# A bidirectional recurrent branch with both directions' gate products first, both roots together and the squares in PSUM

## The chip, the cores and the metric

The kernel is one program on one core of a Trainium2 chip. The metric is the time of one execution on the device, in microseconds (us); less is better. The core's engines run at the same time, each through its own queue in order: PE (TensorE, matrix products), ACT (ScalarE, one function over a tile), DVE (VectorE, elementwise work and scans), POOL (GpSimd) and SP, whose queue issues most transfers. PEld is PE's loading of weights.

## The reference, cut to what matters

One encoder layer over 1024 positions of width 1024: a root-mean-square norm, an input projection, three mixers (a state-space one, a gated linear recurrence called RG-LRU, gated linear attention), three gates, an output projection, then an expert layer of 16 experts and a last norm. The change is in the RG-LRU, 512 channels wide and run in both directions:

```python
def rg_lru_direction(xc, w_a, b_a, w_x, b_x, lam, reverse):
    r = sigmoid(blockdiag(xc, w_a) + b_a)
    i = sigmoid(blockdiag(xc, w_x) + b_x)
    log_a = -LRU_C * r * softplus(-lam)
    a = exp(log_a)
    mult = sqrt(maximum(-expm1(2 * log_a), 0))
    # h[t] = a[t] * h[t-1] + mult[t] * i[t] * xc[t], forwards or backwards in t
    _, h = lax.associative_scan(_lin_combine, (a, mult * (i * xc)), reverse=reverse, axis=1)
    return h

def rg_lru_mixer(xb, ...):
    xc = conv(xb, conv_w, width 4, per channel) + conv_b
    return rg_lru_direction(xc, ..., reverse=False) + rg_lru_direction(xc, ..., reverse=True)
```

## The kernel before

Activations lie with channels on the 128 partitions and the 1024 positions along the free axis. To keep 32-bit accuracy each operand of a large product is split into a high and a low part (`split`: a copy on ACT at L54, a subtraction on DVE at L62), and `mm3` (L68 to L70) adds three products. A projection column of 128 channels (`proj`, L380) takes 48 matmuls into a two-bank PSUM tile `pj`, of which there are two; a branch's way up to the full width (`up`, L390) takes 6 matmuls for each 128 channels of the branch, and 24 for the RG-LRU's 512.

The RG-LRU is a Python generator, `lru_gen`. It goes over four chunks `c` of 128 channels. For a chunk, `lru_conv` loads the row block `xcl`, forms the convolution `xc` on DVE (one multiply, three multiply-adds, one addition of the bias at L897) and splits it into `xch` and `xcl`. Then the body goes over the two directions `d`. A direction has four gate products into `mx` tiles (one PSUM bank each, four of them for the whole program at this stage), four Tanh on ACT into `lr` and `li`, a Tanh into `lt`, an Exp in place over `lr`, a Square into `ls`, on DVE `lt = (ls + 1) * lt` and a maximum with 0 (L928), a square root on ACT, two multiply-adds into `li`, and the scan (L934). `lr` has two buffers; `li`, `lt`, `ls`, `xc`, `xch` and `xcl` have one each. At the end of a chunk the two scans are added and split into the pair `y`, an operand of the way up.

The generator doesn't run alone: `drive(gates_gla, lru_gen(), 6)` writes one task and then six steps of the generator, in turn. The tasks are eight `gla_out` (a gate projection where it isn't there yet, a way up, two DVE passes onto `merged`) and four `ahead_lru` (a gate projection each). The generator has eleven steps for a chunk, so it is written out within the first eight tasks. A list scheduler of the framework then orders each engine's queue: what is written earlier comes first where operands and buffers are ready by its own cost estimates, and what stands under `high_priority` comes before that. After the drive come eight more ways up, for the RG-LRU, which need all four pairs `y`.

ACT holds one table of functions at a time; Tanh, Exp, Square and Copy are served without a load between them here, the square root needs a load before and after it.

Of the kernel before, what the change touches and what calls it, by code (L numbers as in the profile page):

```python
# [8 lines left out]
F32 = mybir.dt.float32  # L9
F32R = mybir.dt.float32r  # L10
BF = mybir.dt.bfloat16
I32 = mybir.dt.int32
AF = mybir.ActivationFunctionType
OP = mybir.AluOpType
# [3 lines left out]
P = 128  # L18
S = 1024
# [18 lines left out]
def dram(t, off, ap):  # L38
    return bass.AP(tensor=t.tensor, offset=t.offset + off, ap=ap)
# [3 lines left out]
def hybrid_encoder(ctx: ExitStack, tc: tile.TileContext, A, out, dbg=None):  # L43
    nc = tc.nc
    v, g, s, te = nc.vector, nc.gpsimd, nc.scalar, nc.tensor
    dma = nc.sync.dma_start
    MUL, ADD, SUB = OP.mult, OP.add, OP.subtract
# [5 lines left out]
    def act(o, i, f, bias=0.0, scale=1.0, **k):  # L53
        return s.activation(o, i, f, bias=bias, scale=scale, **k)  # L54

    def stt(o, a, c, b, op0, op1):
        return v.scalar_tensor_tensor(o, a, c, b, op0=op0, op1=op1)

    def split(h, lo, src, scale=None, eng=None):
        if scale is None:  # L60
            act(h, src, AF.Copy)
            (eng or v).tensor_tensor(lo, src, h.bitcast(F32), SUB)  # L62
        else:
            act(h, src, AF.Copy, scale=scale)
            stt(lo, src, scale, h.bitcast(F32), MUL, SUB)

    def mm3(ps, lh, ll, rh, rl, first, last):
        te.matmul(ps, lh, rl, start=first, stop=False)  # L68
        te.matmul(ps, lh, rh, start=False, stop=False)  # L69
        te.matmul(ps, ll, rh, start=False, stop=last)  # L70
# [16 lines left out]
    def mx():  # L87
        return psum.tile([P, 512], F32, name="mx", bufs=4)
# [11 lines left out]
    def ytile():  # L100
        return ypool.tile([P, S], F32R, name="y")
# [125 lines left out]
    convw, convb = cols[:, 0:16], cols[:, 16:20]  # L227
# [4 lines left out]
    def tt(e, o, a, b, op=MUL):  # L232
        e.tensor_tensor(o, a, b, op)  # L233
# [122 lines left out]
    for n, sg in (("re", 1.0), ("im", -1.0)):  # L356
# [7 lines left out]
        for d in range(2):  # L364
            for t in range(2):
                hs = slice(64 * t, 64 * t + 64)
# [486 lines left out]
    lw = lrctx.enter_context(tc.tile_pool(name="lw", bufs=1, side="right", reuse_waits="tile"))  # L853
# [4 lines left out]
    hba, hbx, hc = (lw.tile(sm, F32, name=n) for n in ("hba", "hbx", "hc"))  # L858
    nhc = l3
# [19 lines left out]
    def lru_conv(c):  # L879

        for i, n in enumerate(("a", "x")):
            for b in range(2):
                bs = slice(64 * b, 64 * b + 64)
                dma(WGr[bs, i::2, bs], dram(A["lru_w_" + n], (2 * c + b) * 4096, [[64, 64], [32768, 2], [1, 64]]))
        WGh = lw.tile([P, 4, P], F32R, name="lwh")
        WGl = lw.tile([P, 4, P], F32R, name="lwl")
        xp = lw.tile([P, S + 3], F32R, name="xcl").bitcast(F32)
        g.memset(xp[:, 0:2], 0.0)
        g.memset(xp[:, S + 2:S + 3], 0.0)
        dma(xp[:, 2:S + 2], LD[c * P:(c + 1) * P])  # L890
        xc = lw.tile([P, S], F32, name="xc")
        v.tensor_scalar(xc, xp[:, 0:S], convw[:, c:c + 1], None, op0=MUL)
        yield
        split(WGh, WGl, WGr)
        for k in range(1, 4):
            stt(xc, xp[:, k:k + S], convw[:, 4 * k + c:4 * k + c + 1], xc, MUL, ADD)
        v.tensor_scalar(xc, xc, convb[:, c:c + 1], None, op0=ADD)  # L897
        yield
        xh = lw.tile([P, S], F32R, name="xch")
        xl = lw.tile([P, S + 3], F32R, name="xcl")[:, 0:S]  # L900
        split(xh, xl, xc)
        yield
        return WGh, WGl, xc, xh, xl

    def lru_gen():
        for c in range(4):
            yield
            WGh, WGl, xc, xh, xl = yield from lru_conv(c)
            hh = []
            for d in range(2):  # L910
                q = slice(4 * d + c, 4 * d + c + 1)
                yield
                rr_ = lw.tile([P, S], F32, name="lr", bufs=2)
                ii_ = lw.tile([P, S], F32, name="li", bufs=1)
                for h in range(2):
                    hs = slice(h * 512, h * 512 + 512)
                    for i, (o_, hb_) in enumerate(((rr_, hba), (ii_, hbx))):
                        ps = mx()
                        mm3(ps, WGh[:, 2 * d + i], WGl[:, 2 * d + i], xh[:, hs], xl[:, hs], True, True)
                        act(o_[:, hs], ps, AF.Tanh, bias=hb_[:, q], scale=0.5)  # L920
                yield
                th = lw.tile([P, S], F32, name="lt", bufs=1)
                act(th, rr_, AF.Tanh, bias=nhc[:, q], scale=nhc[:, q])
                act(rr_, rr_, AF.Exp, bias=hc[:, q], scale=hc[:, q])
                s2 = lw.tile([P, S], F32, name="ls", bufs=1)
                act(s2, rr_, AF.Square)
                stt(th, s2, 1.0, th, ADD, MUL)
                v.tensor_scalar(th, th, 0.0, None, op0=OP.max)  # L928
                act(th, th, AF.Sqrt)
                yield  # L930
                stt(ii_, ii_, 1.0, xc, ADD, MUL)
                stt(ii_, th, 0.5, ii_, MUL, MUL)
                rv = (lambda z: z[:, ::-1]) if d else (lambda z: z)
                v.tensor_tensor_scan(rv(rr_), rv(rr_), rv(ii_), initial=0.0, op0=MUL, op1=ADD)  # L934
                hh.append(rr_)
            yield
            tt(v, hh[0], hh[0], hh[1], ADD)
            if c < 2:
                yh, yl = ytile(), ytile()
            else:  # L940
                yh, yl = (yp2.tile([P, S], F32R, name="y") for _ in range(2))
            split(yh, yl, hh[0])
            ylru.append((yh, yl))
# [6 lines left out]

    gates_gla += [lambda j=j: ahead_lru(j) for j in range(NA)]
    drive(gates_gla, lru_gen(), 6)
    for i, (yh, yl) in enumerate(ylru):
        tap(f"ylruh{i}", yh.bitcast(F32))
# [690 lines left out]
```

## Time and profile before

| | us |
|---|---|
| median of 3 runs (1991.28 to 1994.14) | 1991.97 |
| the profiled execution, its own time | 1994.32 |
| its span in the profile | 1992.5 |
| the recurrent branch, from the first chunk's split `xcl` to the last pair `y` | 474.1 to 623.9 |
| PE's longest wait in this stage | 13.2 |

Times in the rows are microseconds from the span's start. "Idle before" is the time that the engine stood still ahead of an instruction, and the name behind the arrow is the work that released it. The span shows the profiled execution only; runs and profile lie 0.1% apart.

### The profile page before, as it was taken

How to read it: one execution, taken by the hardware profiler on the slowest of the kernel's cores; microseconds unless marked ns; L12 is line 12 of the kernel's file. 1: busy time of each engine (PE TensorE's matmuls, PEld its weight loads, DVE VectorE, ACT ScalarE, POOL GpSimd, SP SyncE). 2: the span in 40 equal slices, each digit the busy share in tenths (PEclk: the TensorE clock that was granted, in tenths of full speed). 3: DMA queues.
4: the chain of work that ended last, by engine and by line, in shares of the span. 5: the costliest groups of instructions: out<-in, count | busy, mean ns of one | idle time of the engine just before them, and what ended most of it. 6: DMA issues, size and time to landing. Idle time of an engine off the chain costs nothing.

```text
span 1992.5 us, 25512 instructions
## 1 busy us (share of the span) xinstructions
PE 1879.4 (94%) x9502; PEld 1542.6 (77%) x9502; DVE 1553.8 (78%) x2018; ACT 1174.8 (59%) x1377; POOL 145.5 (7%) x202
## 2 busy tenths in 40 slices
PE   7989989999997999559999999999999999999995
PEld 6879866777775878448888888888888888888884
DVE  7467235557876243689999999999999999999997
ACT  5121225434665131337778777778777787777785
POOL 0834000000000001000000000000000000000000
PEclk9989999999998999779999999999999999999998
DMA  5432331202212162949999999999999999999992
GB/s 161 111 88 49 96 94 30 83 27 69 69 41 81 32 217 91 337 172 375 385 382 376 393 379 383 390 382 383 381 391 382 381 380 393 378 383 389 384 346 95
DMA packets 263231, 495.95 MB, mean 249 GB/s; under 512 B 26756, under 2 KB 82468, under 8 KB 263108
## 3 DMA queue, kind: packets, MB, share of 16 engines
q1 hardware_dynamic: 255924, 468.64, 65.2%
q0 software_dynamic: 7184, 25.69, 4.3%
q8 instruction: 74, 1.21, 0.3%
q14 instruction: 49, 0.40, 0.1%
HBM read 464.55 MB, written 29.74 MB: 248 GB/s over the span
## 4 chain that ended last, share of the span: by engine, by line
PE 80%; DVE 6%; ACT 3%; issue 1%; DMA 1%; SPq 0%; POOLq 0%; DVEq 0%; ACTq 0%
PE py L1447 17%; PE pj L380 12%; PE gu L68 12%; PE gu L70 12%; PE gu L69 12%; PE pj L390 3%; PE tp L1403 2%; PE mo L68 2%; PE mo L69 1%; PE mo L70 1%; DVE junk L1317 1%; DVE lr L934 0%; PE mx L795 0%; PE mx L802 0%; ACT gt L54 0%
## 5 line engine op out<-in xcount | busy, mean ns | idle before, releaser
L233 DVE TENSOR_TENSOR xwl<-rawb,xwh 128x1024 fp32r<-128x1024 f32 x528 | 614.0, 1220 | 19.8 <-ACT xwh L54 18.8
L54 ACT ACTIVATE xwh<-rawb 128x1024 fp32r<-128x1024 f32 x528 | 522.1, 1053 | 13.6 <-PE gu L70 7.0
L68 PE MATMUL gu<-xwl,xeh 128*128 128x512 f32 x1024 | 406.2, 397 | 0.0
L70 PE MATMUL gu<-xwh,xel 128*128 128x512 f32 x1024 | 399.9, 391 | 0.0
L69 PE MATMUL gu<-xwh,xeh 128*128 128x512 f32 x1024 | 399.3, 390 | 0.0
L233 DVE TENSOR_TENSOR xwl<-rawa,xwh 128x1024 fp32r<-128x1024 f32 x192 | 226.2, 1220 | 15.3 <-ACT xwh L54 15.2
L70 PEld LDWEIGHTS gu<-xwh,xel 128*128 128x128 f32 x1024 | 192.3, 188 | 41.0 <-DVE xel L62 0.2
L69 PEld LDWEIGHTS gu<-xwh,xeh 128*128 128x128 f32 x1024 | 192.6, 188 | 38.0
L68 PEld LDWEIGHTS gu<-xwl,xeh 128*128 128x128 f32 x1024 | 192.6, 188 | 37.7 <-ACT xeh L54 0.2
L54 ACT ACTIVATE xwh<-rawa 128x1024 fp32r<-128x1024 f32 x192 | 193.0, 1054 | 7.1 <-PE py L1447 7.1
L380 PE MATMUL pj<-xnL,wh 128*128 128x512 f32 x576 | 181.3, 394 | 3.5 <-ACT ev L54 1.9
L380 PE MATMUL pj<-xnH,wl 128*128 128x512 f32 x576 | 180.8, 393 | 0.0
L380 PE MATMUL pj<-xnH,wh 128*128 128x512 f32 x576 | 180.4, 392 | 0.0
L1447 PE MATMUL py<-xwl,hTh 128*128 128x512 f32 x512 | 159.8, 393 | 2.3 <-DVE xwl L233 2.3
L54 ACT ACTIVATE wh<-wraw 128x1024 fp32r<-128x1024 f32 (+2 forms) x60 | 49.6, 828 | 189.5 <-PE pj L380 129.1
L1447 PE MATMUL py<-xwh,hTl 128*128 128x512 f32 x512 | 158.7, 391 | 0.4 <-DVE hTl L62 0.4
L1447 PE MATMUL py<-xwh,hTh 128*128 128x512 f32 x512 | 158.3, 390 | 0.0
L62 DVE TENSOR_TENSOR wl<-wraw,wh 128x1024 fp32r<-128x1024 f32 (+2 forms) x60 | 57.6, 962 | 104.5 <-ACT wh L54 89.9
L380 PEld LDWEIGHTS pj<-xnL,wh 128*128 128x128 f32 x576 | 107.1, 188 | 29.5 <-ACT ev L54 3.0
L380 PEld LDWEIGHTS pj<-xnH,wl 128*128 128x128 f32 x576 | 107.2, 188 | 25.6 <-issue 2.1
L380 PEld LDWEIGHTS pj<-xnH,wh 128*128 128x128 f32 x576 | 107.9, 188 | 24.5 <-issue 1.8
L1447 PEld LDWEIGHTS py<-xwh,hTl 128*128 128x128 f32 x512 | 96.4, 188 | 21.1 <-DVE hTl L62 0.9
(472 smaller groups left out, 2539.9 us busy)
## 6 DMA issues: line engine op xcount, KB each, us to landing
rawb<-in_w_exp_down_dram SPq DMA_DIRECT2D x90, 1024.0 KB, 8.8
rawb<-in_w_exp_up_dram SPq DMA_DIRECT2D x88, 1024.0 KB, 8.3
rawb<-in_w_exp_gate_dram SPq DMA_DIRECT2D x86, 1024.0 KB, 8.9
rawa<-in_w_exp_up_dram SPq DMA_DIRECT2D x40, 1024.0 KB
rawa<-in_w_exp_gate_dram SPq DMA_DIRECT2D x33, 1024.0 KB
rawa<-in_w_exp_down_dram SPq DMA_DIRECT2D x23, 1024.0 KB
wraw<-in_w_in_dram SPq DMA_DIRECT2D x36, 512.0 KB, 4.0
rawc<-in_w_exp_down_dram SPq DMA_DIRECT2D x15, 1024.0 KB
```

Of the source, the lines that this page charges most:

```text
L54: return s.activation(o, i, f, bias=bias, scale=scale, **k)
L62: (eng or v).tensor_tensor(lo, src, h.bitcast(F32), SUB)
L68: te.matmul(ps, lh, rl, start=first, stop=False)
L69: te.matmul(ps, lh, rh, start=False, stop=False)
L70: te.matmul(ps, ll, rh, start=False, stop=last)
L233: e.tensor_tensor(o, a, b, op)
L380: te.matmul(ps[:, h], w[:, k], xx[:, k, h * 512:(h + 1) * 512], start=(k == 0 and i == 0), stop=(k == KT - 1 and i == 2))
L390: te.matmul(ps[:, h], ww[:, k], yy[:, h * 512:(h + 1) * 512], start=(k == 0 and i == 0), stop=(k == len(ys) - 1 and i == 2))
L1317: v.tensor_scalar(junk[:, half_], PT[:, half_], cand.bitcast(F32), 0.0, op0=OP.is_ge, op1=ADD, accum_out=cnt)
L1403: te.transpose(ps[:, j * P:(j + 1) * P], src[:, j * P:(j + 1) * P], idn)
L1447: te.matmul(E.py[:, h], a[:, j], b[:, h * 512:(h + 1) * 512], start=(f == 0 and j == 0 and p_ == 0), stop=(f == 3 and j == 3 and p_ == 2))
```

## The change

- The bias of the convolution moves into its first pass (a multiply and an addition in one `tensor_scalar`); the separate pass at L897 goes.
- The gate products of both directions, and their eight Tanh, are written out before anything else of the chunk; `li` gets a second buffer for this.
- The Tanh, Exp and Square of both directions follow, then both square roots next to each other, then the multiply-adds and scans of both directions.
- The Square goes to PSUM in two halves of 512 positions, each into an `mx` tile, and the multiply-add that reads it is halved too. The tile `ls` goes.
- The `lt` of the second direction lies in the buffer of `xch`, which is therefore held until that direction's last multiply-add.
- The number of generator steps for a chunk stays eleven.

```diff
-        v.tensor_scalar(xc, xp[:, 0:S], convw[:, c:c + 1], None, op0=MUL)
+        v.tensor_scalar(xc, xp[:, 0:S], convw[:, c:c + 1], convb[:, c:c + 1], op0=MUL, op1=ADD)
         yield
         split(WGh, WGl, WGr)
         for k in range(1, 4):
             stt(xc, xp[:, k:k + S], convw[:, 4 * k + c:4 * k + c + 1], xc, MUL, ADD)
-        v.tensor_scalar(xc, xc, convb[:, c:c + 1], None, op0=ADD)
...
-            hh = []
+            hh, gi, gm = [], [], []
             for d in range(2):
                 q = slice(4 * d + c, 4 * d + c + 1)
                 yield
                 rr_ = lw.tile([P, S], F32, name="lr", bufs=2)
-                ii_ = lw.tile([P, S], F32, name="li", bufs=1)
+                ii_ = lw.tile([P, S], F32, name="li", bufs=2)
...
+                hh.append(rr_)
+                gi.append(ii_)
+            yield
+            for d in range(2):
+                q = slice(4 * d + c, 4 * d + c + 1)
+                th = lw.tile([P, S], F32R, name="xch").bitcast(F32) if d else lw.tile([P, S], F32, name="lt")
+                act(th, hh[d], AF.Tanh, bias=nhc[:, q], scale=nhc[:, q])
+                act(hh[d], hh[d], AF.Exp, bias=hc[:, q], scale=hc[:, q])
+                stt(gi[d], gi[d], 1.0, xc, ADD, MUL)
+                for h in range(2):
+                    hs = slice(h * 512, h * 512 + 512)
+                    s2 = mx()
+                    act(s2, hh[d][:, hs], AF.Square)
+                    stt(th[:, hs], s2, 1.0, th[:, hs], ADD, MUL)
+                v.tensor_scalar(th, th, 0.0, None, op0=OP.max)
+                gm.append(th)
                 yield
-                th = lw.tile([P, S], F32, name="lt", bufs=1)
-                act(th, rr_, AF.Tanh, bias=nhc[:, q], scale=nhc[:, q])
-                act(rr_, rr_, AF.Exp, bias=hc[:, q], scale=hc[:, q])
-                s2 = lw.tile([P, S], F32, name="ls", bufs=1)
-                act(s2, rr_, AF.Square)
-                stt(th, s2, 1.0, th, ADD, MUL)
-                v.tensor_scalar(th, th, 0.0, None, op0=OP.max)
-                act(th, th, AF.Sqrt)
-                yield
-                stt(ii_, ii_, 1.0, xc, ADD, MUL)
-                stt(ii_, th, 0.5, ii_, MUL, MUL)
+            for d in range(2):
+                act(gm[d], gm[d], AF.Sqrt)
+            yield
+            for d in range(2):
+                stt(gi[d], gm[d], 0.5, gi[d], MUL, MUL)
                 rv = (lambda z: z[:, ::-1]) if d else (lambda z: z)
-                v.tensor_tensor_scan(rv(rr_), rv(rr_), rv(ii_), initial=0.0, op0=MUL, op1=ADD)
-                hh.append(rr_)
+                v.tensor_tensor_scan(rv(hh[d]), rv(hh[d]), rv(gi[d]), initial=0.0, op0=MUL, op1=ADD)
```

## Rows read from the trace of the kernel before

**Rows 1.** The page's chain of work that ended last, by engine

```profile
PE 80%; DVE 6%; ACT 3%; issue 1%; DMA 1%; SPq 0%; POOLq 0%; DVEq 0%; ACTq 0%
```

**Rows 2.** Busy time by stretch: stretch, length, busy us (instructions) by engine, granted clock, DMA

```profile
519.00:555.00 36.00, 34.74 (x150) 27.92 (x150) 27.32 (x26) 24.63 (x27) 0.14 (x2) 1.00 0.29 77
...
611.00:624.00 13.00, 0.09 (x1) 0.09 (x1) 9.11 (x7) 5.96 (x6) 0.00 (x0) 0.69 0.00 0
624.00:629.20 5.20, 5.20 (x13) 4.04 (x14) 1.82 (x2) 1.25 (x2) 0.00 (x0) 0.50 0.00 0
629.20:706.00 76.80, 76.57 (x337) 63.06 (x335) 28.05 (x28) 16.28 (x19) 1.05 (x11) 1.00 0.24 70
```

**Rows 3.** PE's waits, 440 to 760 us: total, times, longest

```profile
PE pj L390 <- DVE y L62: 13.2, 1, 13.2
...
PE mx L68 <- DVE xcl L62: 2.5, 2, 1.8
```

**Rows 4.** DVE in order of time, 460 to 690 us: start, duration, line, tiles

```profile
472.85 1.22 DVE L62 TENSOR_TENSOR xcl<-xc,xch 128x1024 fp32r<-128x1024 f32 x1 [0.44 <-ACT xch L54]
...
517.90 1.22 DVE L62 TENSOR_TENSOR xcl<-xc,xch 128x1024 fp32r<-128x1024 f32 x1
...
538.50 1.23 DVE L57 SCALAR_TENSOR_TENSOR li<-li,xc 128x1024 f32<-128x1024 f32 x1 [1.33 <-ACT li L54]
539.82 0.75 DVE L892 TENSOR_SCALAR xc<-xcl,cols 128x1024 f32<-128x1024 f32 x1
...
551.61 0.75 DVE L897 TENSOR_SCALAR xc<-xc,cols 128x1024 f32<-128x1024 f32 x1
...
554.48 1.20 DVE L62 TENSOR_TENSOR xcl<-xc,xch 128x1024 fp32r<-128x1024 f32 x1
...
590.07 1.22 DVE L62 TENSOR_TENSOR xcl<-xc,xch 128x1024 fp32r<-128x1024 f32 x1
...
622.63 1.22 DVE L62 TENSOR_TENSOR y<-lr,y 128x1024 fp32r<-128x1024 f32 x1 [1.12 <-ACT y L54]
```

**Rows 5.** ACT's groups by form, 455 to 626 us: count, busy, mean ns, idle before

```profile
L54 ACT ACT_TABLE_LOAD x15 | 19.2, 1283 | 4.0 <-DVE lr L934 3.7
...
L54 ACT ACTIVATE li<-mx,hbx 128x512 f32<-128x512 f32 x16 | 10.5, 682 | 3.2 <-DVE lr L934 3.2
L54 ACT ACTIVATE lt<-lr,l 128x1024 f32<-128x1024 f32 x8 | 10.0, 1247 | 0.1
...
L54 ACT ACTIVATE ls<-lr 128x1024 f32<-128x1024 f32 x8 | 8.5, 1062 | 0.1
L54 ACT ACTIVATE lt<-lt 128x1024 f32<-128x1024 f32 x8 | 8.5, 1060 | 4.9 <-DVE lt L928 4.8
```

**Rows 6.** DVE's groups by form, 455 to 626 us

```profile
L934 DVE TENSOR_TENSOR_SCAN lr<-lr,li 128x1024 f32<-128x1024 f32 x8 | 18.3, 2288 | 0.1
L57 DVE SCALAR_TENSOR_TENSOR xc<-xcl,cols,xc 128x1024 f32<-128x1024 f32 x12 | 15.4, 1283 | 0.2
...
L57 DVE SCALAR_TENSOR_TENSOR lt<-ls,lt 128x1024 f32<-128x1024 f32 x8 | 9.8, 1224 | 8.9 <-ACT ls L54 8.9
...
L928 DVE TENSOR_SCALAR lt<-lt 128x1024 f32<-128x1024 f32 x8 | 5.5, 690 | 0.1
...
L897 DVE TENSOR_SCALAR xc<-xc,cols 128x1024 f32<-128x1024 f32 x4 | 3.0, 752 | 0.0
```

**Rows 7.** DVE's groups by form, 250 to 460 us: a half-width pass on PSUM

```profile
L57 DVE SCALAR_TENSOR_TENSOR gt<-mx,cols,gt 128x512 f32<-128x512 f32 x4 | 2.8, 746 | 0.2
```

**Rows 8.** ACT in order of time, 460 to 680 us

```profile
475.12 0.69 ACT L54 ACTIVATE lr<-mx,hba 128x512 f32<-128x512 f32 x1 [2.31 <-PE mx L70]
...
487.97 1.06 ACT L54 ACTIVATE lt<-lt 128x1024 f32<-128x1024 f32 x1 [1.71 <-DVE lt L928]
489.04 1.28 ACT L54 ACT_TABLE_LOAD   x1
```

**Rows 9.** The waits of SP's queue, 455 to 626 us

```profile
SPq L890 <- PE mx L68: 16.1, 3, 10.1
```

## Prediction

> **What bounds the kernel now.** I read the page's chain of work first: 80% of the span is PE's own work [rows 1], so time is won here only where PE stands still or runs slowly. Second, PE's waits around the recurrent branch: one wait of 13.2 us, of a way up for the last pair `y`, and 2.5 us in two waits for a chunk's split `xcl` [rows 3]. The reader should see that PE has used up all other work there: its filler (gate projections, the ways up of the first three pairs) ends at about 610.7 us, which is 13.2 us ahead of the end of the last `y` at 622.63 + 1.22 = 623.9 us [rows 3, 4]. Third, busy time by stretch. From 611 to 624 us PE is idle and the granted clock falls; from 624.0 to 629.2 us PE is busy throughout at 0.50, the lower level of 1.2 GHz; from 629.2 us to 706 us it is busy 76.57 of 76.80 us at 1.00 [rows 2]. So the late `y` costs 13.2 us of standing still and 5.2 x (1 - 0.50) = 2.6 us of half speed, and nothing behind it gives that back: PE is full at once. With the waits for `xcl` at most 13.2 + 2.6 + 2.5 = 18.3 us can be won.
>
> Fourth, why `y` is late. The split `xcl` ends at 474.1, 519.1, 555.7 and 591.3 us, the last `y` at 623.9 us [rows 4]: four chunks, one after the other, of 45.0, 36.6, 35.6 and 32.6 us. In chunk 1 the second direction's `li` reaches DVE only at 538.5 us, 19.4 us after its `xcl`, since `li` has one buffer and its Tanh waits for the first scan (the 3.2 us in ACT's `li` group) [rows 4, 5]. Only then is `xc` free, and the next convolution, 5.35 us of work (0.75 + 3 x 1.28 + 0.75), starts at 539.8 us and ends at 552.4 us, squeezed between the second direction's passes and the tasks' [rows 4, 6]. DVE is busy 27.3 of 36 us in this stretch [rows 2], but idle early in a chunk and full late.
>
> **The change part by part.** ACT, per chunk: four table loads become two if both roots stay together; 15 lie in the stage [rows 5], about 8 go, 8 x 1.28 = 10.3 us. The trace has the next load 0.01 us behind a root that ends at 489.03 us, and nothing else between [rows 8]. The Trainium skill ("ScalarE: Activation LUTs", What ACT_TABLE_LOAD costs) puts some 1.38 us of drain on top of each switch; by it 21.3 us would go, but these rows don't show that part, so I leave it out. The sum goes by 10.3 us; most of it is shadowed by waits for DVE, and it counts only in the chain below.
>
> The halved squares write to PSUM, which no row of ACT shows. Bounds for one half: half of the 1.06 us of `ls`, 0.53, and the 0.68 us of a half-width Tanh that reads PSUM [rows 5]. I take 0.60, between them: +0.14 us a direction, +1.1 us in all (0 to +2.4). The multiply-add on a half: 0.61 (half of 1.224) to 0.746, the one half-width row that reads PSUM [rows 6, 7]. I take the latter: +0.27 us a direction, +2.1 us in all (0 to 2.1). The bias in the first pass of the convolution: a two-step pass isn't in the trace; as one pass at 0.75 us it saves 0.75 us a chunk, 3.0 us in all, as two it saves nothing. I take 3.0. DVE's sum is thus -0.9 us (-3.0 to +2.1): its load does not change.
>
> What changes is the order. Walk through a chunk, from the end of `xcl`: 1.05 us until the first Tanh (474.07 to 475.12) [rows 4, 8]; eight Tanh at 0.68 = 5.4; two Tanh and two Exp at 1.25 = 5.0 (Exp taken like the Tanh); four half squares = 2.4; a load 1.28; a root 1.06 [rows 5]. That is 16.2 us. Both maxima (0.69 each) lie beside ACT's work, the second one beside the load and the first root. Then DVE: two multiply-adds at 1.22 and two scans at 2.29 = 7.0, the addition 1.22, and for `y` 1.06 on ACT and 1.22 on DVE [rows 4 to 6]: 26.7 us to the end of `y`. The same sum over the old order's dependences is 1.05 + 4 x 0.68 + 2 x 1.25 + 1.06 + 1.22 + 0.69 + 1.06 + 1.22 + 2.29 = 13.8 us to the first scan's end, then 2 x 0.68 + 1.25 + 1.06 + 1.22 + 0.69 + 1.06 + 1.22 + 2.29 = 10.2, and 3.5 for the rest: 27.5 us, of which the last chunk took 32.6, so 5.1 us are the neighbours' work. As a bare chain the new order is hardly shorter. I take the last chunk at 1 to 3 us less.
>
> The gain is in the hand-over to the next chunk. `xc` is now free when the second direction's first multiply-add has run, about 1.05 + 5.4 + 1.2 = 7.7 us after `xcl`, where it was 19.4 + 1.2 = 20.6 us. So the convolution runs while ACT works and DVE has gaps, instead of between the scans. What comes last is `xch`: its buffer is held by the second `lt` until that direction's last multiply-add, 16.2 + 1.22 + 2.29 + 1.22 = 20.9 us; then the split's 1.06 on ACT beside the second scan, and 1.22 on DVE behind it: 20.9 + 2.29 + 1.22 = 24.4 us from `xcl` to `xcl`. With the same 5.1 us for neighbours a chunk takes 29.5 us, against 36.6 and 35.6, and against 45.0 in the first, which also shared its start with the attention branch. That is 6 to 7 us for each of three chunks, more in the first, and 1 to 3 in the last: 20 to 24 us, if all goes through. DVE bounds this: its own work of a chunk is 22.8 us (5.35 - 0.75 for the convolution, two directions of 1.22 + 1.49 + 0.69 + 1.22 + 2.29, 1.22 for the addition, 1.22 for each of two splits, some 0.7 for the split of the weights), with 5.1 us of tasks 27.9 of 29.5: nearly full, so a part of that gain may be lost to order.
>
> SP's queue is in order, and the load of the next `xcl` (L890) waits there 16.1 us in three times for the last gate product, with the tasks' weight loads behind it [rows 9]. The eight products now come in one row, so it is released no later; the weights' loads behind it gain. POOL's two memsets go the same way. Of PSUM, the four squares of a chunk take `mx` tiles between this chunk's products and the next one's.
>
> **The sum.** The branch must end by about 610.7 - 2.5 = 608 us for PE never to wait: 16 us earlier. Three quarters of 20 to 24 us, 15 to 18, nearly do that. I take a rest of 1.5 us, PE's waits for `xcl` as they are, and the lower clock gone: 13.2 + 2.6 - 1.5 = 14.3 us. The profiled execution would take 1994.3 - 14.3 = 1980.0 us, and the runs, whose median lies 2.3 us below it, 1977.7, say 1978 us.
>
> **The rivals.** A measurement of this kernel can tell about 0.2%, 4 us, from no change.
> 1. Half shortened: the scheduler squeezes DVE's passes as before, each chunk wins 2 to 3 us, and PE still waits 5 to 8 us, with a lower clock behind it. Gain 4 to 10 us: 1982 to 1988 us. For it speaks that DVE is nearly full by my sum; against it the first chunk's 45.0 us.
> 2. The branch's end stays: as the bare chains show, 26.7 against 27.5 us, the last chunk alone wins nothing, and if DVE's order loses what the hand-over wins, the 13.2 us remain: 1988 to 1996 us. Against it: `xc` is freed some 13 us earlier whatever the order.
> 3. Slower: PE's queue is fixed when the program is built. If the scheduler puts a chunk's products ahead of filler because it expects `xcl` sooner than the held `xch` allows, PE stands behind them. It decides from 18.3 / 3 = 6.1 us at each of three hand-overs; at 8 us each, 24 us, and some 2.6 us of half speed behind them, less the 18.3: 2000 us. Against it: these waits sum to 2.5 us now [rows 3].
> 4. Products wait on squares. `mx` has four tiles: if four products of a chunk each wait for a half square and its multiply-add, 0.60 + 0.75 = 1.35 us, that is 5.4 us a chunk and 21.6 us in four, less the 14.3 won: 1999 us. Against it: a chunk's products are written ahead of its squares, and the next one's come 10 us later. The Trainium skill ("ScalarE: Activation LUTs", the note on PSUM as a destination under Step-by-step) calls PSUM the faster side for ACT, but only useful if TensorE doesn't need most of it; no row here shows either.
>
> **How the numbers follow.** Forecast (gain of 10 to 18.3 us, 1973 to 1982): 0.56. Rival 1: 0.20. Rival 2: 0.12. Rival 3: 0.09. Rival 4: 0.03. Faster by over 0.2% is the forecast and rival 1, 0.76; within 0.2% rival 2, 0.12; slower 0.12. The range starts at 1972.5, the 18.3 us and a little for a shorter first chunk, and must reach through most of rival 1 to leave out no more than 2 in 10: 1988.
>
> **What would show it.** Right: PE's wait for `y` under 3 us or gone, no stretch at 0.50 behind it, hand-overs of some 30 us, about 7 table loads in the stage, the convolution between the first Tanh and the roots. A half square over 0.68 us or a half multiply-add over 0.75 would break those terms. Wrong: PE waits of several us for `xcl` (rival 3) or on `mx` behind squares (rival 4), or 13 us for `y` still (rival 2).

## The result, and the profile after

The changed kernel takes 1981.92 us, the median of four runs (1980.58 to 1983.27), against 1993.06 us (1991.28 to 1994.60) for the kernel before in the same comparison: a ratio of 0.9946, 95% interval 0.9934 to 0.9958, which is 11.1 us less (8.4 to 13.2). Forecast were 1978 us and a gain of 14.3 us; the time lies in the range from 1972.5 to 1988 us, the gain came out 3 us short. The profiled execution took 1980.58 us with a span of 1978.8 us.

Two profiles can't be subtracted whole: the last transpose of the attention branch (L828), which stands ahead of all that the change touches, starts at 450.8 us before and 447.3 us after, so 3.5 us of the difference of the profiles were there already (the last section says where they come from). From here on, the **stage** is the stretch from that transpose to the first product of the output projection (L68 into `mo`), and its length is what is compared. It goes from 257.7 us (450.8 to 708.5) to 248.4 us: 9.3 us, which lies within the interval of the gain.

Busy time by stretch after: stretch, length, busy us (instructions) of PE, PEld, DVE, ACT, POOL, granted clock, DMA. These answer to [rows 2].

```profile
447.30:695.70 248.40, 236.40 (x1024) 191.55 (x1022) 154.98 (x172) 118.13 (x145) 1.58 (x19) 0.99 0.22 60
...
532.00:564.00 32.00, 29.29 (x126) 23.50 (x126) 29.06 (x29) 22.83 (x27) 0.13 (x2) 1.00 0.31 82
564.00:570.00 6.00, 5.57 (x17) 4.43 (x18) 2.73 (x3) 3.03 (x4) 0.00 (x0) 0.72 0.00 0
598.00:628.00 30.00, 30.00 (x134) 24.85 (x133) 13.41 (x15) 8.61 (x10) 0.00 (x0) 1.00 0.38 100
```

PE is now busy throughout where the last pair `y` arrives (598 to 628 us, at 1.00), where it stood still for 13 us and ran at 0.50 for 5.2 us before [rows 2]. In their place there is a new stretch at 0.72, from 564 to 570 us. The whole stage before had 237.87 us of PE's work in its 257.7 us, so PE stood idle for 19.8 us of it; now it is 12.0 us. PE's waits after, 440 to 760 us (total, times, longest), against [rows 3]:

```profile
PE mx L68 <- DVE xcl L62: 6.5, 3, 2.6
PE mo L68 <- ACT MH L54: 3.0, 2, 2.7
PE pj L390 <- DVE ev L57: 2.1, 2, 1.2
PE pj L380 <- ACT ev L54: 0.6, 2, 0.3
```

The wait for `y` (13.2 us) is gone, not shortened. The waits for `xcl` went from 2.5 to 6.5 us, and two for `ev`, the pass that frees a `pj` tile, are new. PE in order of time shows the three waits for `xcl`, one at each hand-over from chunk to chunk, and the first way up of the last pair:

```profile
502.63 0.50 PE L68 MATMUL mx<-xcl,lwh 128*128 128x512 f32 x1 [1.36 <-DVE xcl L62]
...
532.22 0.50 PE L68 MATMUL mx<-xcl,lwh 128*128 128x512 f32 x1 [2.55 <-DVE xcl L62]
...
564.43 0.57 PE L68 MATMUL mx<-xcl,lwh 128*128 128x512 f32 x1 [2.60 <-DVE xcl L62]
564.79 0.63 PE L69 MATMUL mx<-xch,lwh 128*128 128x512 f32 x1
...
568.18 0.39 PE L68 MATMUL mx<-xcl,lwh 128*128 128x512 f32 x1
...
605.72 1.07 PE L390 MATMUL pj<-y,wh 128*128 128x512 f32 x4
```

Behind the third wait a matmul takes 0.63 us instead of 0.39 until 568.2 us: 3.8 us at the lower clock of 1.2 GHz, which cost half of that, 1.9 us. The first way up of the last pair starts at 605.7 us, 7.3 us after `y` is ready. DVE in order of time, beside [rows 4]:

```profile
468.66 1.23 DVE L62 TENSOR_TENSOR xcl<-xc,xch 128x1024 fp32r<-128x1024 f32 x1 [0.24 <-ACT xch L54]
...
477.20 1.23 DVE L57 SCALAR_TENSOR_TENSOR li<-li,xc 128x1024 f32<-128x1024 f32 x1 [1.08 <-ACT li L54]
...
482.08 0.81 DVE L892 TENSOR_SCALAR xc<-xcl,cols 128x1024 f32<-128x1024 f32 x1
...
497.98 1.28 DVE L57 SCALAR_TENSOR_TENSOR xc<-xcl,cols,xc 128x1024 f32<-128x1024 f32 x1
...
501.38 1.20 DVE L62 TENSOR_TENSOR xcl<-xc,xch 128x1024 fp32r<-128x1024 f32 x1
...
530.96 1.20 DVE L62 TENSOR_TENSOR xcl<-xc,xch 128x1024 fp32r<-128x1024 f32 x1
...
563.17 1.20 DVE L62 TENSOR_TENSOR xcl<-xc,xch 128x1024 fp32r<-128x1024 f32 x1
...
597.21 1.22 DVE L62 TENSOR_TENSOR y<-lr,y 128x1024 fp32r<-128x1024 f32 x1 [1.13 <-ACT y L54]
```

The splits end at 469.9, 502.6, 532.2 and 564.4 us, the last `y` at 598.4: chunks of 32.7, 29.6, 32.2 and 34.1 us where they took 45.0, 36.6, 35.6 and 32.6. The branch takes 128.5 us instead of 149.8. ACT's groups after, 455 to 626 us (count, busy, mean ns, idle before), beside [rows 5], and DVE's, beside [rows 6, 7]:

```profile
L54 ACT ACT_TABLE_LOAD x10 | 12.8, 1283 | 0.2
...
L54 ACT ACTIVATE mx<-lr 128x512 f32<-128x512 f32 x16 | 8.9, 602 | 0.0
...
L54 ACT ACTIVATE xch<-xc 128x1024 fp32r<-128x1024 f32 x4 | 4.2, 1062 | 21.5 <-DVE xc L57 19.1 <-DVE li L57 2.4
```

```profile
L57 DVE SCALAR_TENSOR_TENSOR lt<-mx,lt 128x512 f32<-128x512 f32 x8 | 5.1, 683 | 3.8 <-ACT mx L54 3.8
...
L892 DVE TENSOR_SCALAR xc<-xcl,cols 128x1024 f32<-128x1024 f32 x4 | 3.2, 811 | 3.2 <-DMA xcl<-LD 3.2
```

### The profile page after: what moved, and what is told of

The parts are those of the page before. It is cut to its first block, busy times and chain, and to the rows that moved or that the text cites. A ratio compares the mean times of both kernels' runs of the same rounds, so it can differ in the third digit from the quotient of the medians.

```text
span 1978.8 us, 25510 instructions
## 1 busy us (share of the span) xinstructions
PE 1874.6 (95%) x9502; PEld 1539.2 (78%) x9502; DVE 1549.6 (78%) x2022; ACT 1165.8 (59%) x1379; POOL 145.1 (7%) x202
## 4 chain that ended last, share of the span: by engine, by line
PE 80%; DVE 7%; ACT 2%; issue 1%; DMA 1%; POOLq 0%; DVEq 0%; ACTq 0%
PE py L1455 17%; PE pj L380 12%; PE gu L68 12%; PE gu L70 12%; PE gu L69 12%; PE pj L390 3%; PE tp L1411 2%; PE mo L68 2%; PE mo L70 1%; PE mo L69 1%; DVE lr L943 1%; DVE junk L1325 1%; PE mx L795 0%; PE mx L802 0%; PE mx L68 0%
## 5 line engine op out<-in xcount | busy, mean ns | idle before, releaser
L233 DVE TENSOR_TENSOR xwl<-rawb,xwh 128x1024 fp32r<-128x1024 f32 x528 | 613.7, 1218 | 19.8 <-ACT xwh L54 18.8
L68 PE MATMUL gu<-xwl,xeh 128*128 128x512 f32 x1024 | 406.2, 397 | 0.0
L233 DVE TENSOR_TENSOR xwl<-rawa,xwh 128x1024 fp32r<-128x1024 f32 x192 | 226.1, 1219 | 15.4 <-ACT xwh L54 15.4
L68 PEld LDWEIGHTS gu<-xwl,xeh 128*128 128x128 f32 x1024 | 192.6, 188 | 37.7 <-ACT xeh L54 0.2
```

## The experiments

Each kernel of an experiment ran beside the kernel before on the same chip, whose medians there lay between 1991.5 and 1992.9 us, so ratios are compared and not times. "Stage" is the length as above, "idle" that length less PE's busy time in it, "branch" from the end of the first split `xcl` to that of the last `y`, "loads" ACT's table loads from 455 to 626 us, and the last two columns are PE's waits. Each stage is read from a single profiled execution. What a kernel saves by its stage and by its ratio differs by up to 2.4 us (e9_li2_bias_products: 11.5 us of stage, 13.9 us of time), so a smaller difference between two stages shows nothing by itself.

| kernel | median us | ratio [95%] | stage | idle | branch | loads | wait `y` | wait `xcl` |
|---|---|---|---|---|---|---|---|---|
| before | 1993.06 | 1 | 257.7 | 19.8 | 149.8 | 15 | 13.2 | 2.5 |
| after | 1981.92 | 0.9946 [0.9934, 0.9958] | 248.4 | 12.0 | 128.5 | 10 | 0 | 6.5 |
| e1_bias | 1986.06 | 0.9973 [0.9961, 0.9985] | 251.7 | 14.5 | 145.7 | 15 | 7.1 | 1.0 |
| e6_sq_only | 1984.76 | 0.9962 [0.9949, 0.9976] | 250.9 | 13.5 | 143.5 | 15 | 8.0 | 0.6 |
| e2_li2 | 1975.63 | 0.9917 [0.9903, 0.9930] | 240.6 | 6.2 | 133.1 | 16 | 0.9 | 0 |
| e5_li2_bias | 1975.06 | 0.9913 [0.9898, 0.9929] | 240.5 | 6.1 | 133.0 | 16 | 0 | 1.5 |
| e4_li1 | 1988.40 | 0.9982 [0.9973, 0.9991] | 253.6 | 15.4 | 146.4 | 8 | 9.3 | 1.6 |
| e3_roots | 1981.10 | 0.9945 [0.9931, 0.9958] | 248.3 | 11.8 | 128.4 | 10 | 0 | 5.7 |
| e7_li2_held | 1978.15 | 0.9928 [0.9915, 0.9942] | 243.6 | 8.9 | 136.7 | 16 | 0 | 1.6 |
| e8_li2_products | 1979.41 | 0.9934 [0.9921, 0.9948] | 244.3 | 8.4 | 138.8 | 15 | 2.6 | 0.7 |
| e9_li2_bias_products | 1978.59 | 0.9930 [0.9916, 0.9943] | 246.2 | 8.6 | 140.1 | 15 | 2.6 | 0 |
| e10_li2_bias_held | 1974.83 | 0.9915 [0.9901, 0.9928] | 242.3 | 8.0 | 136.2 | 16 | 0 | 4.2 |
| e11_after_not_held | 1982.76 | 0.9949 [0.9936, 0.9963] | 245.8 | 10.5 | 130.1 | 8 | 0 | 4.1 |
| e12_after_4_steps | 1980.58 | 0.9946 [0.9932, 0.9959] | 245.6 | 9.8 | 132.5 | 8 | 0 | 3.9 |

**The bias alone** (e1_bias: the kernel before, with the bias in the first pass).

```diff
-        v.tensor_scalar(xc, xp[:, 0:S], convw[:, c:c + 1], None, op0=MUL)
+        v.tensor_scalar(xc, xp[:, 0:S], convw[:, c:c + 1], convb[:, c:c + 1], op0=MUL, op1=ADD)
...
-        v.tensor_scalar(xc, xc, convb[:, c:c + 1], None, op0=ADD)
```

> The kernel before with the convolution's bias in its first pass and nothing else. Theory A (the gain is the earlier hand-over of xc to the next chunk): 0.75 us a chunk come off, the last pair y ends up to 3 us earlier, PE's wait for it goes from 13.2 to about 10 us, the time falls by 0 to 4 us. Theory B (DVE's load bounds the branch, so the pass that goes is a large part of the gain): 5 us or more.

PE's waits in this kernel:

```profile
PE pj L390 <- DVE y L62: 7.1, 1, 7.1
...
PE mx L68 <- DVE xcl L62: 1.0, 2, 0.7
```

Four passes less, 2.8 us of DVE's work (4 x 0.752 for the bias, less the longer first pass, 4 x 0.06), and PE waits 6.1 us less for `y`; the stage is 6.0 us shorter. The time falls by 5.4 us (3.0 to 7.8), which is in Theory B's range. It doesn't prove Theory B: the pass counted for more than its own length, but the order behind it shifted too (the chunks took 33.9, 47.5, 28.0 and 36.3 us).

**The squares and the second `li`, in the old order** (e2_li2, with the separate bias).

```diff
-                ii_ = lw.tile([P, S], F32, name="li", bufs=1)
+                ii_ = lw.tile([P, S], F32, name="li", bufs=2)
...
-                s2 = lw.tile([P, S], F32, name="ls", bufs=1)
-                act(s2, rr_, AF.Square)
-                stt(th, s2, 1.0, th, ADD, MUL)
+                for h in range(2):
+                    hs = slice(h * 512, h * 512 + 512)
+                    s2 = mx()
+                    act(s2, rr_[:, hs], AF.Square)
+                    stt(th[:, hs], s2, 1.0, th[:, hs], ADD, MUL)
```

> The kernel before with the second buffer of li and the halved squares in PSUM, in the old order of writing, bias pass and separate roots kept. Theory A: the second direction's li no longer waits for the first scan, xc is free some 8 to 10 us earlier, PE's wait for y falls below half of 13.2 us and the time by 6 to 11 us. Rival C (it needs both directions' products and roots together): less than 4 us.

The stage's busy time, PE's wait and ACT's loads in this kernel, three views:

```profile
450.00:690.60 240.60, 234.38 (x1023) 190.56 (x1021) 158.64 (x175) 128.61 (x151) 1.58 (x19) 1.00 0.22 62
```

```profile
PE pj L390 <- DVE y L62: 0.9, 1, 0.9
```

```profile
L54 ACT ACT_TABLE_LOAD x16 | 20.5, 1283 | 0.3
```

With 16 loads, in the old order, the kernel is faster than the changed one: the intervals of the two ratios don't meet. It gains 15.8 us, more than the 6 to 11 of Theory A. So neither fewer loads nor the new order is what the change lives by. The wait for `y` is nearly gone, and PE's clock is 1.00 over the whole stage.

**The roots apart again** (e3_roots: the changed kernel, each root written right behind its maximum).

```diff
                 v.tensor_scalar(th, th, 0.0, None, op0=OP.max)
+                act(th, th, AF.Sqrt)
...
-            for d in range(2):
-                act(gm[d], gm[d], AF.Sqrt)
```

> The changed kernel with each direction's root straight behind its maximum, so that about 16 table loads stand in the stage instead of 10. Theory A: the loads are off the path, y still ends before PE's other work does, the time stays within 3 us of the changed kernel's 1982. Theory D (the gain is the saved loads): 6 to 10 us of 11 come back, 1988 to 1992. Theory E (loads make the real chunk later than PE's fixed order expects): PE's waits for xcl grow from 6.5 us by 2 us or more for each of three hand-overs.

The edit did not produce what it was to produce: ACT's and DVE's rows in the branch stand in the same order as in the changed kernel, with 10 loads. For these two ways of writing the framework's scheduler made the same order. The run shows only that writing the roots together has no effect of its own here; no run changes the roots' grouping alone, and what fewer loads are worth can only be read from e2_li2 and e11_after_not_held. As a repeat of the same order it shows how far a stage is reproduced: 248.3 against 248.4 us, with waits for `xcl` of 5.7 and 6.5 us.

**One `li`** (e4_li1: the changed kernel with the old single buffer).

```diff
-                ii_ = lw.tile([P, S], F32, name="li", bufs=2)
+                ii_ = lw.tile([P, S], F32, name="li", bufs=1)
```

> The changed kernel with one buffer of li. Theory A: the second direction's li waits for the first scan again and xc with it, the hand-overs go back from 30 to 33 us to 35 us or more, PE waits for y again by 5 us or more, the time is 1988 us or more. Rival C: the new order alone carries the gain, 1980 to 1985 us.

```profile
PE pj L390 <- DVE y L62: 9.3, 1, 9.3
```

PE's wait for `y` is back, as Theory A has it, with only 8 loads, and the stage is 5.2 us longer than the changed kernel's. The second buffer is a necessary part.

**The best parts together** (e5_li2_bias: e2_li2 with the bias of e1_bias).

> The second buffer of li and the halved squares in the old order, and the bias in the convolution's first pass as well. If PE is the bound once its wait for y is gone (0.9 us of it was left without the bias pass), the pass saves at most what PE still waits: 1973 to 1976 us. If DVE's load still sets the pace, another 3 to 5 us: 1970 to 1973.

```profile
446.90:687.40 240.50, 234.41 (x1024) 190.57 (x1022) 156.75 (x172) 128.86 (x151) 1.58 (x19) 1.00 0.22 62
```

The stage is as long as in e2_li2 within 0.1 us. The bias that was worth 6.0 us alone is worth nothing that can be measured once PE hardly waits for `y`: of the 6.1 us of idle time that are left, 2.7 are the wait for `MH` behind the branch. With e2_li2, and with e10_li2_bias_held below, this is a version that beats both kernels: the intervals of these three don't meet the changed kernel's.

**The squares alone** (e6_sq_only: the kernel before with only the second part of e2_li2's diff).

> The kernel before with the halved squares in PSUM and nothing else. Theory A (the second buffer is the cause of the gain): within 3 us of the kernel before, PE's wait for y 11 to 16 us. Rival F (the halves let DVE start on the first half while ACT squares the second): 5 us or more faster.

DVE's waits for the Tanh into `li` and for the squares (`lt`), first in the kernel before (there the squares' wait is 8.9 us, [rows 6]), then in this one:

```profile
DVE li L57 <- ACT li L54: 15.8, 7, 5.0
```

```profile
DVE li L57 <- ACT li L54: 8.6, 5, 5.0
...
DVE lt L57 <- ACT mx L54: 3.9, 3, 1.8
```

I had costed this part as a small loss, as more passes; it shortens the stage by 6.8 us, as Rival F expected. DVE's wait ahead of the multiply-add falls from 8.9 to 3.9 us. In four of the eight cases DVE starts while ACT still squares the second half (at 517.96 us, for instance, with the squares running from 517.33 to 518.45 us). But the order shifts too: the wait for `li` falls by 7.2 us although nothing in its code changed. How much of the 6.8 us the early start is worth isn't shown; that the passes themselves are no cheaper is (a pair of halves takes 1.12 us on ACT and 1.28 us on DVE, the whole tile 1.06 and 1.22). The second `li` on top of it (e2_li2 against e6_sq_only) gives 10.3 us more.

**What in the new order costs time** (e7_li2_held: e2_li2 with the second `lt` in the buffer of `xch`; e8_li2_products: e2_li2 with the products of both directions first; e9_li2_bias_products and e10_li2_bias_held: the same two edits on e5_li2_bias).

```diff
-                th = lw.tile([P, S], F32, name="lt", bufs=1)
+                th = lw.tile([P, S], F32R, name="xch").bitcast(F32) if d else lw.tile([P, S], F32, name="lt", bufs=1)
```

```diff
-            hh = []
+            hh, pr = [], []
...
+                pr.append((rr_, ii_))
+            for d in range(2):
+                q = slice(4 * d + c, 4 * d + c + 1)
+                rr_, ii_ = pr[d]
```

> The second buffer and the halved squares in the old order, with the second direction's lt in the buffer of xch as the change has it. Theory G (the held xch delays the next chunk's split and PE stands in front of it): PE's waits for xcl come to 4 us or more and the time to 1979 or more. Rival H (the products of both directions in one row are what costs): no waits for xcl, 1974 to 1977.

> The second buffer and the halved squares, the gate products of both directions first, the rest of each direction in the old order with one buffer of lt. Theory H (the products in one row are what costs): PE's waits for xcl come to 4 us or more, 1979 to 1984 us. Theory G (the held xch costs): no such waits, 1974 to 1977 us.

> The second buffer, the halved squares and the fused bias, with the gate products of both directions first and each direction's rest in the old order with one buffer of lt. If the products in one row are the larger part of what the changed kernel loses: 1979 to 1983 us, PE's waits in the branch (xcl, ev, y) at 5 us or more. If the held xch is: 1974 to 1977 us.

> The second buffer, the halved squares and the fused bias in the old order, with the second direction's lt in the buffer of xch. If the held xch is the larger part of what the changed kernel loses: 1979 to 1983 us with waits for xcl of 4 us or more. If the products in one row are: 1975 to 1978 us.

PE's wait for `y` in e9_li2_bias_products and the stretch behind it, then the waits for `xcl` in e10_li2_bias_held:

```profile
PE pj L390 <- DVE y L62: 2.6, 1, 2.6
```

```profile
609.10:615.00 5.90, 5.80 (x18) 4.63 (x19) 3.24 (x5) 1.26 (x2) 0.00 (x0) 0.71 0.15 37
```

```profile
PE mx L68 <- DVE xcl L62: 4.2, 3, 1.8
```

None of the four came out as a theory had it. e7_li2_held waits 1.6 us for `xcl` and takes 1978.2 us, between G and H. e8_li2_products takes H's time, but without the waits for `xcl` that were to bring it; e9_li2_bias_products takes 1978.6 us, between its two, with 3.2 us of waits for `xcl`, `ev` and `y`. e10_li2_bias_held has the waits (4.2 us) without the time. On the stage each edit costs something on either base: the held buffer 3.0 and 1.8 us, the products first 3.7 and 5.7 us; the 1.8 us alone would show nothing. The waits differ. With the buffer held, PE waits for `xcl` and `ev` (3.5 and 5.1 us in the two), as in the changed kernel. With the products first and one `lt`, the branch itself becomes longer than in its base (138.8 against 133.1 us, 140.1 against 133.0), and PE waits 2.6 us for `y`. Behind this wait e9_li2_bias_products runs slowly, 5.9 x (1 - 0.71) = 1.7 us of its 5.7, and e8_li2_products doesn't (last section). The sum, 5.7 + 1.8 = 7.5 us, is near the 7.9 us between the changed kernel's stage and e5_li2_bias's, but since the changed kernel has no wait for `y`, this near sum is no proof of two parts. In the ratios none of the four differs from its base by more than the intervals leave open; the changed kernel, with both edits and the new order, does.

**The buffer not held, in the new order** (e11_after_not_held: the changed kernel; in chunks 0 and 1 the second `lt` lies in a `y` buffer that is still free).

```diff
-                th = lw.tile([P, S], F32R, name="xch").bitcast(F32) if d else lw.tile([P, S], F32, name="lt")
+                th = (ytile() if c < 2 else lw.tile([P, S], F32R, name="xch")).bitcast(F32) if d else lw.tile([P, S], F32, name="lt")
```

> The changed kernel with the second direction's lt of chunks 0 and 1 in a free buffer of y instead of that of xch, so that two of the three hand-overs are free of the hold. If the hold makes PE wait for xcl: that wait falls from 6.5 to about 2.6 us and the time to 1977 to 1980. If the convolution's last passes on DVE do (ACT's xch waits 19.1 us for them and 2.4 us for the hold): it stays at 5 us or more, 1980 to 1984 us.

```profile
PE mx L68 <- DVE xcl L62: 4.1, 3, 2.1
```

The three waits in order of time:

```profile
505.61 0.50 PE L68 MATMUL mx<-xcl,lwh 128*128 128x512 f32 x1 [1.31 <-DVE xcl L62]
...
541.11 0.50 PE L68 MATMUL mx<-xcl,lwh 128*128 128x512 f32 x1 [0.72 <-DVE xcl L62]
...
574.98 0.50 PE L68 MATMUL mx<-xcl,lwh 128*128 128x512 f32 x1 [2.07 <-DVE xcl L62]
```

The waits come to 4.1 us, between what the theories expected; the time of 1982.8 us is in the second one's range. The stage is 2.6 us shorter, but the ratio is the changed kernel's within its interval, so a gain isn't shown. The hold is gone at the first two hand-overs. The first wait stays (1.31 against 1.36 us), so it isn't the hold's. The second falls (0.72 against 2.55), but its chunk takes 35.5 us instead of 29.6, so the order shifted with it, and how much of this wait was the hold's isn't shown. The kernel also has the 8 loads that the change was to bring, and isn't measurably faster for them.

**Fewer steps for each task** (e12_after_4_steps: the changed kernel with four generator steps for a task, so that more filler is written between the products of two chunks).

```diff
-    drive(gates_gla, lru_gen(), 6)
+    drive(gates_gla, lru_gen(), 4)
```

> The changed kernel with four steps of the generator written after each task instead of six, which leaves PE's queue as it is up to chunk 2's first direction, and puts 60 matmuls of other work between chunk 2's two directions, so that chunk 3's products stand 14 us later in it. Theory J (PE stands in front of xcl because its queue has the products ahead of other work that is ready): the third wait for xcl (2.6 us) and the half speed behind it (some 2 us) go, the first two stay (3.9 us), y ends some 10 us later but still about in time for PE, 1976 to 1980 us. Rival K (the waits follow from the chain, wherever the products stand): the waits for xcl stay at 6 us or more, 1981 to 1985 us.

PE's waits, and PE in order of time at the second and the third hand-over:

```profile
PE mx L68 <- DVE xcl L62: 3.9, 2, 2.5
...
PE pj L390 <- DVE ev L57: 2.8, 2, 1.9
```

```profile
531.93 0.80 PE L68 MATMUL mx<-xcl,lwh 128*128 128x512 f32 x1 [2.55 <-DVE xcl L62]
532.52 0.63 PE L69 MATMUL mx<-xch,lwh 128*128 128x512 f32 x1
...
574.55 0.39 PE L68 MATMUL mx<-xcl,lwh 128*128 128x512 f32 x1
```

The third wait for `xcl` is gone, with its slow stretch: the split ends at 572.6 us, its first product comes at 574.6 us behind filler, at full speed, although the split is 8 us later than in the changed kernel. The second wait stays, and now it is this one that PE runs slowly behind (0.63 us a matmul). The stage is 2.8 us shorter, the ratio unchanged; the time of 1980.6 us lies between the two theories, the waits are as J has them. So at this hand-over the place of the products in PE's queue decided whether a late `xcl` cost time; moved in one place of three it isn't worth what the runs can tell.

## Why the prediction came out as it did

**The bound and the 15.8 us.** Right. The late `y` was what could be won: its 13.2 us of waiting and the 2.6 us of half speed behind it [rows 2, 3] are both gone.

**The rest of 1.5 us.** Too cautious: no wait for `y` is left; PE comes to it 7.3 us after it is ready. The branch ended 21.3 us sooner after its first split, within the 20 to 24 us, where the sum had trusted three quarters of that. That this total was met is luck in part. The first chunk gave 12.3 us (45.0 to 32.7), where the sum counted little more than 6 to 7; the next two gave 7.0 and 3.4 us, and the last, taken at 1 to 3 us less, took 1.5 us more: its first Tanh came 3.5 us after its split (567.91 against 564.37 us), where the walk had 1.05, behind products at the lower clock and a table load.

**The step that was off: "PE's waits for `xcl` as they are".** They measured 6.5 us instead of 2.5, 4.0 more. Not in the sum at all were the waits for `ev` (2.1 us) and the slow stretch behind the third `xcl` (3.8 us at half speed, 1.9 us). 13.2 + 2.6 - 4.0 - 2.1 - 1.9 = 7.8 us; the stage shows 9.3. Of the rest of 1.5 us the small waits explain 0.5 (0.8 and 0.3 us for `lwh` and `li` are gone, those for `MH` and ACT's `ev` grew by 0.3 each); the other 1.0 us stays open. The forecast of 14.3 us was thus 1.5 us too low for `y` and 8.0 us too high for what came in its place. This is rival 3 in small: 1.3 to 2.6 us at a hand-over, where it needed 6.1 to decide. e2_li2 and e5_li2_bias, in the old order, have 0 and 2.3 us of the waits for `xcl` and `ev` and no slow stretch (1.00 over the stage), and e12_after_4_steps removes one by moving the products.

**The hand-over.** Forecast 29.5 us, measured 32.7, 29.6 and 32.2. `xc` came free at 8.5 us after the split (477.20 + 1.23 against 469.9), as walked (7.7). But at the first and the third hand-over `xch` isn't what comes last: ACT's copy waits for the last pass of the convolution. (Of the 21.5 us in ACT's group 19.1 are such waits, 7.3 of them ahead of the first chunk, where there is no hold.) ACT in order of time, the copy at each hand-over:

```profile
499.36 1.06 ACT L54 ACTIVATE xch<-xc 128x1024 fp32r<-128x1024 f32 x1 [5.83 <-DVE xc L57]
...
526.70 1.06 ACT L54 ACTIVATE xch<-xc 128x1024 fp32r<-128x1024 f32 x1 [2.40 <-DVE li L57]
...
561.15 1.06 ACT L54 ACTIVATE xch<-xc 128x1024 fp32r<-128x1024 f32 x1 [5.91 <-DVE xc L57]
```

The convolution's first pass starts at 482.08 and the last ends at 499.26 us, 17 us for four passes that take 4.7 us together, as the tasks' passes and the direction's own stand between them. In the second chunk, where the convolution is done at 524.4 us, `xch` does come last (freed at 526.7 us), and the walk's 29.5 us are met to 0.1 us, though not step by step: `xch` is free 24.1 us after the split, where the walk had 20.9, and both scans come behind it, where the walk had one. By these rows the hold cost at most 526.7 - 524.4 = 2.3 us there. The first passes also wait 3.2 us for the load of the next `xcl`, which SP issues behind the last gate product: hidden before, where `xc` came free later, and not in the sum.

**Loads.** Forecast were about 8 fewer than 15, some 7 left; found were 10: in the third chunk a task's pass with a load of its own stands between the two roots. No run shows that loads are worth time here (e2_li2 with 16, e11_after_not_held with 8). A load takes 1283 ns; a copy ends at 552.86 us, the next load starts at 552.88, and the root behind it at 554.17. The Trainium skill ("ScalarE: Activation LUTs", What ACT_TABLE_LOAD costs) states these 1283 ns and some 1.38 us of drain on top for each switch; the trace agrees on the load, and the drain is again not in the rows.

**Sizes.** A half square 0.602 us (forecast 0.60), a half multiply-add 0.68 (0.746), the first pass with the bias 0.811 (0.75). The halving was priced as work added, +3.2 us; that it would shorten the stage, by 6.8 us when made alone (e6_sq_only), was not seen.

**Rivals.** 1 and 2 fell with the wait for `y`. The time alone doesn't part the forecast from rival 1: the measured gain, 8.4 to 13.2 us, reaches into the 4 to 10 us of rival 1. It is the missing wait that does. 4 fell too: among PE's waits after there is none on `mx` for a square.

**What is shown and what isn't.** Shown: the halved squares and the bias shorten the stage each alone (e6_sq_only, e1_bias), the second `li` does on top of the squares and within the new order (e2_li2, e4_li1), and squares and second `li` together all but free PE; the change's new order then loses 7.9 us of stage against e5_li2_bias, although its branch is shorter (128.5 against 133.0 us). By PE's rows this loss lies in 5.0 us more of waits for `xcl`, 1.3 us more for `ev` and the 1.9 us at the lower clock. Open: how it divides between the products first, the held buffer and the rest of the new order, and why the scheduler places the products where it does. Not tried were the second `li` alone, full-width squares beside it, halved squares in SBUF, so that halves and PSUM aren't told apart, and a buffer of its own for the second `lt` in all chunks.

## What to carry to other kernels

Shorten a side branch until the engine that bounds the kernel no longer waits for it, and stop there: the same pass was worth 6.0 us while PE waited and nothing afterwards, and the reordering that made the branch shorter still lost time at its hand-overs, where PE's fixed queue met operands that came 1 to 3 us late. Try the small edits alone first: here a second buffer and squares in halves gave more without the reordering around them than with it. Compare the stretch that the change touches, between two events outside of it, rather than whole spans.

## What the runs showed of the hardware that was not expected

Ahead of the branch, where the kernels are written alike, PE ran at a different granted clock from one profile to the next. The window of 125 to 150 us, first of the kernel before, then of the changed one:

```profile
125.00:150.00 25.00, 20.68 (x161) 18.72 (x162) 11.42 (x16) 3.72 (x7) 8.85 (x10) 0.80 0.23 61
```

```profile
125.00:150.00 25.00, 21.90 (x187) 19.99 (x188) 14.81 (x25) 4.32 (x9) 8.85 (x10) 0.93 0.27 76
```

Of the fourteen profiles eight show 0.80 here, four 0.93 and two 0.86. Each is one execution of another kernel, so they don't part the execution from the kernel; but the mean granted clock of the whole span differs between the four executions of the changed kernel too, from 0.979 for a span of 1978.8 us to 0.977 for 1981.5. As an estimate, (0.93 - 0.80) x 25 = 3.3 us, nearly the whole 3.5 us by which the two profiles differ ahead of the branch.

A wait of 2.60 us for `xcl` at 564 us was followed by 3.8 us at the lower level of 1.2 GHz; one of 2.55 us at 532 us in the same profile by none (granted clock 1.00 from 532 to 564 us). In e3_roots, where ACT's and DVE's rows stand in the same order, it is the other way round: the second wait, 2.56 us, was followed by the lower level, the third, 1.77 us, was not. And of two kernels in which PE waits 2.58 us for the last `y` at the same place, e9_li2_bias_products ran at 0.71 behind it (its stretch of 5.9 us above) and e8_li2_products at 1.00. Behind the wait in e3_roots, then behind the one in e8_li2_products:

```profile
535.00:541.00 6.00, 5.22 (x16) 4.15 (x17) 6.00 (x7) 3.48 (x5) 0.00 (x0) 0.72 0.12 26
```

```profile
612.80:618.70 5.90, 5.77 (x24) 4.47 (x25) 4.15 (x6) 1.26 (x2) 0.00 (x0) 1.00 0.20 45
```

The length of the wait alone doesn't tell which comes, so the 1.9 us that the changed kernel lost in this way can't be put down to its order alone.
